# One stacked matmul for the gates' end tiles, transposes moved among the second halves, and a deeper lookahead

## The chip, the cores and the metric

The kernel runs on one core of a Trainium2 chip. The metric is the device time of one execution in microseconds. The kernel before took 1441.75 us (median of three runs, 1441.58 to 1443.41).

## The reference

The input is one sequence of 256 tokens of width 1024, in fp32. Two blocks follow one another, each two layers deep.

Each layer of the first block computes `proj = rmsnorm(x) @ w_in` and splits it for three branches: a gated spatial MLP (a), a latent attention (b) and a gated linear recurrence (c). Each branch's output is projected back to 1024 columns, multiplied by a sigmoid gate (`g_a`, `g_b`, `g_c`) and added up; the sum goes through `w_out` and a norm into the residual. The recurrence, which most of the change touches, is:

```python
r = sigmoid(blockdiag(xc, w_a) + b_a);  i = sigmoid(blockdiag(xc, w_x) + b_x)   # 16 blocks of 80 x 80
a = exp(-8 * r * softplus(-lam));       b = sqrt(1 - a*a) * (i * xc)
h[t] = a[t] * h[t-1] + b[t]             # along the 256 tokens;  y_c = h * silu(z_c)
```

The second block has a pooling mixer (first layer) or a sparse attention (second layer), then a convolutional feed-forward of inner width 2816, then a gate: `x = x + sigmoid(rmsnorm(x) @ ple_gate) * (p @ ple_proj)`. A last norm ends it.

## The kernel before, in words

**Arithmetic.** Every fp32 matrix product is made of three matmuls of rounded fp32 parts: `mm3` (L479 to L483) adds hi*hi, hi*lo and lo*hi. A product is either token-major (`tok_halves`, L569: the activations are stationary, 512 columns of weights stream; the 256 tokens are two halves of 128) or feature-major (`feat_tile`: the weights are stationary, 256 tokens stream).

**Weights.** All weights lie in one DRAM array in the order of use, in chunks of up to 512 KB. The class `Stream` loads them: `get` (L382) for chunk i first issues the loads up to chunk i + `raw_ahead` (3) and the splits up to i + `split_ahead` (2). A split (L364) is one ScalarE copy to `hi` (L376) and one VectorE subtraction per 512 columns to `lo` (L379). There are 4 raw buffers and 7 pairs of hi and lo; a raw buffer is free when VectorE has made its `lo`. All loads are issued by SyncE.

**Order.** The framework's scheduler takes the instructions of each engine mostly in the order in which the program gives them, lets a ready one pass one that waits (by its own model of time), and adds all semaphores. On the chip each engine then runs its list in order.

**Recurrence gates (`gates`, L944).** The 1280 channels are 10 tiles of 128, in two periods of 5 tiles, and the blocks of 80 straddle tiles. For each period, each of two gates and each of 5 tiles, there is one `mm3` on the tile itself and one on an `edge` operand with the neighbours' rows: 64 rows of the tile before and 64 of the one after, copied by GpSimd (L936) into `es` tiles. The two end tiles of a period (0 and 4) have one neighbour in the period, and take that neighbour's whole tile as `edge`. `MERGE_ORDER` runs branch a's gate and projection for one half of the columns (`ga`, `pa`), `gates(0)`, the other half, `gates(1)`.

**After the gates.** Both halves of the third gate's product (`gc`, on `hT`) come next; then VectorE squares `av` (L985), takes the minimum with 1 (L986), ScalarE the root (L987); VectorE multiplies (L989) and scans along the tokens (L992). Then `zc` (10 feature tiles, each pair with a silu at L617, L618, a product with the scan's result at L1001, and a split into `yc` at L491 and L492), then the projection `pc` on `yc` in two column halves of 5 chunks each.

**Feed-forward, gate, and their norms.** `ffn` ends with the last 7 inner tiles of the down product, half 0 of the tokens and then half 1. Then come, for each half, the residual (L1165), the next norm's product and sum of squares (L555, L512), eight transposes (L538, in the helper `transpose_split`) and the split into the next stage's `hT` (L488, L489). `tok_pair` (L579) computes the 1024-wide products with six chunks held, half 0 ahead of half 1; `ple` does its residual after it in the same manner.

Of the kernel before, what the change touches and what calls it, by code (L numbers as in the profile page):

```python
# [187 lines left out]
FFN_TAIL = 7  # L188
PAIR_HELD = 6
# [229 lines left out]
class Net:  # L419
# [59 lines left out]
    def mm3(self, ps, a, b, start, stop):  # L479
        mm = self.nc.tensor.matmul  # L480
        mm(ps, a[0], b[0], start=start, stop=False)  # L481
        mm(ps, a[0], b[1], start=False, stop=False)  # L482
        mm(ps, a[1], b[0], start=False, stop=stop)  # L483
# [59 lines left out]
    def norm(self, *key, dst=None, rs=None, fold=None):  # L543


        gain = self.row(*key)
        dst = dst or self.feat4("hT", KD)
        run_rs = rs or [None, None]

        def run(half):  # L550
            if fold:
                hs = self.u2s("h", 2)
                for n, h in enumerate(hs):
                    cs = slice(n * 512, (n + 1) * 512)
                    self.nc.vector.tensor_tensor(h, self.x[half][:, cs], gain[n], op=ALU.mult)  # L555
            if run_rs[half] is None:
                run_rs[half] = self.rs_x(half, fold or 1.0)
            if not fold:
                hs = self.scaled_x(half, run_rs[half], gain)
            for n, h in enumerate(hs):  # L560
                self.transpose_split(h, dst, half, 4 * n, 4)

        run.dst, self.rs = dst, run_rs
# [15 lines left out]
    def tok_pair(self, key, f):  # L579

        ps = [[self.psA(), self.psA()] for _ in range(2)]
        def part(half, i, w):
            n, c = divmod(i, 4)
            for k in range(2):
                kg = 2 * c + k
                self.mm3(ps[n][half], f.pair(kg, half), (w[0][:, k, :], w[1][:, k, :]), kg == 0, kg == KD - 1)

        def get(i):
            return self.w.get((*key, i // 4, i % 4), 512)

        ws = [get(i) for i in range(PAIR_HELD)]
        for i in range(PAIR_HELD):
            part(0, i, ws[i])
        for i in range(8 - PAIR_HELD):
            part(1, i, ws[i])
            ws.append(get(PAIR_HELD + i))
            part(0, PAIR_HELD + i, ws[-1])
        for i in range(8 - PAIR_HELD, 8):
            part(1, i, ws[i])
        return ps  # L600
# [132 lines left out]
    def first_layer(self, l):  # L733
# [119 lines left out]
        for n in range(2):  # L853
            ps = self.tok_group(("v", l, n), hT)
# [23 lines left out]
        for n in range(2):  # L878
            ps = self.tok_group(("u", l, n), hT)
            for half in range(2):  # L880
                nc.vector.tensor_tensor(sv[half][n], sv[half][n], ps[half], op=ALU.mult)
            heads(4 + 2 * n, 5 + 2 * n)
        ya = self.feat4("ya", 8)
        for n in range(2):
            ps = self.tok_group(("za", l, n), hT)
# [58 lines left out]
        def gates(p):  # L944
# [5 lines left out]
            for gi in range(2):  # L950
                pvs = []
                for mi in range(5):
# [6 lines left out]
                    self.mm3(pv, w[1], edge[mi], False, True)  # L959
# [14 lines left out]

        for kind, i in MERGE_ORDER:
# [4 lines left out]
        tg = [gate("gc", n) for n in range(2)]  # L980
# [135 lines left out]
    def ffn(self, l):  # L1116
# [26 lines left out]

        def down(*js):
            ws = [self.w.get(("down", l, j), 512) for j in js]
            for half in range(2):
                sl = slice(half * P, half * P + P)
                for j, (wh, wl) in zip(js, ws):
                    f = act[j]
                    for n in range(2):  # L1150
                        self.mm3(acc[half][n], (f[:, 0, sl], f[:, 1, sl]), (wh[:, n, :], wl[:, n, :]),
                                 j == 0, j == KF - 1)
# [8 lines left out]
        down(*range(KF - FFN_TAIL, KF))  # L1161
        for half in range(2):
# [3 lines left out]
            nxt(half)  # L1166
# [8 lines left out]
    def ple_in(self, l, n):  # L1175
        if n == 0:
            self.pp = [[], []]
        ps = self.tok_group(("pp", l, n), self.pf, kts=2)
# [5 lines left out]
    def ple(self, l):  # L1184
# [5 lines left out]
        pss = self.tok_pair(("pg", l), hT)  # L1190
        for half in range(2):
            for n in range(2):
                cs = slice(n * 512, n * 512 + 512)
                t = self.tmp()
                nc.scalar.activation(t, pss[n][half], AF.Tanh, scale=rs[half])
                nc.vector.scalar_tensor_tensor(t, t, 1.0, self.pp[half][n], op0=ALU.add, op1=ALU.mult)
                nc.vector.tensor_tensor(self.x[half][:, cs], self.x[half][:, cs], t, op=ALU.add)
            nxt(half)
# [15 lines left out]
    def nsa(self):  # L1214
# [15 lines left out]
        ps = self.tok_group(("kv", 0), h1)  # L1230
# [72 lines left out]
        def keys_values(s):  # L1303
            ps = self.tok_group(("kv", 1 + s), h1)
# [43 lines left out]
        def queries(n):  # L1348
            ps = self.tok_group(("qb", n), hT)
# [206 lines left out]
```

## Time and profile before

| | |
|---|---|
| median of 3 runs | 1441.75 us |
| profiled execution | 1441.76 us |
| its span, first to last instruction | 1440.0 us |
| TensorE / VectorE / ScalarE / GpSimd busy | 97% / 73% / 59% / 6% |
| granted TensorE clock, mean | 0.994 |
| DMA | 249.32 MB, mean 173 GB/s |
| chain that ended last | TensorE 81%, VectorE 9%, ScalarE 5%, DMA 3% |

The busy time of TensorE overstates its rate: a matmul's row gives its time from start to end, and the next one starts before that end. The pace is read from the starts in the timeline.

### The profile page before, as it was taken

To read this page: it belongs to the slowest core of one execution; us is meant where nothing else is said; L and a number is where in the kernel's file an instruction comes from. 1 tells how busy PE (TensorE), PEld (TensorE's weight loads), DVE (VectorE), ACT (ScalarE), POOL (GpSimd) and SP (SyncE) were. 2 spreads that over 40 slices of the span, in tenths; PEclk is the share of its full clock that TensorE was granted. 3 is DMA by queue.
4 is the path that set the end of the run, shared out by engine and by line. 5 is a ranking of instruction groups with operands and counts; after the bars stand their busy time and mean duration, and the time that the engine had idled before them with its cause. 6 is when DMAs were issued, how large, how long until landed. Compare 5 with 4: busy or idle time off the path is not lost.

```text
span 1440.0 us, 23026 instructions
## 1 busy us (share of the span) xinstructions
PE 1399.3 (97%) x8506; PEld 1236.1 (86%) x8506; DVE 1049.4 (73%) x2131; ACT 844.6 (59%) x1421; POOL 92.0 (6%) x155
## 2 busy tenths in 40 slices
PE   6999999999999999999999999999999999999997
PEld 6987889889789878898897899999888778999985
DVE  7856748659767676577687688777696788787765
ACT  6665545656455665456655466555565796665554
POOL 1000002100010000021000000000010440000000
PEclk9999999999999999999999999999999999999999
DMA  8553555564646634665656555555555115655652
GB/s 282 183 196 117 163 188 190 168 214 136 228 139 207 214 118 129 194 201 161 203 175 231 163 181 186 191 178 189 183 172 171 50 38 189 194 180 189 188 164 86
DMA packets 73408, 249.32 MB, mean 173 GB/s; under 512 B 8272, under 2 KB 8912, under 8 KB 73296
## 3 DMA queue, kind: packets, MB, share of 16 engines
q1 hardware_dynamic: 72576, 245.95, 52.1%
q10 hardware_dynamic: 720, 1.91, 0.5%
q8 instruction: 67, 1.10, 0.3%
q14 instruction: 45, 0.37, 0.1%
HBM read 246.77 MB, written 1.05 MB: 172 GB/s over the span
## 4 chain that ended last, share of the span: by engine, by line
PE 81%; DVE 9%; ACT 5%; DMA 3%; issue 2%; POOL 1%; POOLq 0%; ACTq 0%; DVEq 0%; SPq 0%
PE psA L481 22%; PE psA L483 22%; PE psA L482 22%; PE psB L481 3%; DVE lo L379 3%; PE psB L482 3%; DMA raw<-in_w_dram 3%; PE psB L483 3%; ACT hi L376 2%; PE psB L538 1%; ACT es L1415 1%; DVE av L992 1%; POOL rs L502 1%; PE psB L1054 1%; PE psB L1036 1%
## 5 line engine op out<-in xcount | busy, mean ns | idle before, releaser
L379 DVE TENSOR_TENSOR lo<-raw,hi 128x512 fp32r<-128x512 f32 (+2 forms) x897 | 585.0, 679 | 221.3 <-ACT hi L376 215.8
L376 ACT ACTIVATE hi<-raw 128x1024 fp32r<-128x1024 f32 (+3 forms) x449 | 467.6, 1045 | 309.8 <-PE psA L483 112.3
L482 PE MATMUL psA<-hT,hi 128*128 128x256 f32 x1160 | 328.6, 283 | 0.5 <-DVE hT L489 0.5
L483 PE MATMUL psA<-hT,lo 128*128 128x256 f32 x1160 | 328.2, 283 | 0.0
L481 PE MATMUL psA<-hT,hi 128*128 128x256 f32 x1160 | 328.1, 283 | 0.0
L481 PE MATMUL psA<-hi,hT 128*128 128x512 f32 (+2 forms) x592 | 230.6, 390 | 3.2 <-ACT hT L488 3.2
L482 PE MATMUL psA<-lo,hT 128*128 128x512 f32 (+2 forms) x592 | 228.5, 386 | 1.4 <-DVE lo L379 1.4
L483 PE MATMUL psA<-hi,hT 128*128 128x512 f32 (+2 forms) x592 | 229.1, 388 | 0.0
L482 PEld LDWEIGHTS psA<-hT,hi 128*128 128x128 f32 x1160 | 221.9, 191 | 2.0 <-DVE hT L489 0.7
L481 PEld LDWEIGHTS psA<-hT,hi 128*128 128x128 f32 x1160 | 221.8, 191 | 1.6 <-ACT hT L488 0.2
L483 PEld LDWEIGHTS psA<-hT,lo 128*128 128x128 f32 x1160 | 221.9, 191 | 0.0
L481 PEld LDWEIGHTS psA<-hi,hT 128*128 128x128 f32 x592 | 111.8, 189 | 22.6 <-ACT hT L488 4.1
L482 PEld LDWEIGHTS psA<-lo,hT 128*128 128x128 f32 x592 | 111.5, 188 | 21.4 <-DVE lo L379 2.1
L483 PEld LDWEIGHTS psA<-hi,hT 128*128 128x128 f32 x592 | 111.5, 188 | 20.4 <-DVE hT L489 0.5
L502 POOL TENSOR_TENSOR rs<-ms,mhalf 128x1 f32<-128x1 f32 x34 | 28.3, 832 | 977.1 <-DVE ms L501 788.1
L1135 DVE SCALAR_TENSOR_TENSOR tmp<-psA,colt,tmp 128x255 f32<-128x255 f32 (+1 forms) x176 | 84.2, 478 | 1.2
L481 PE MATMUL psB<-hi,fact 128*128 128x512 f32 x176 | 68.8, 391 | 0.0
L482 PE MATMUL psB<-lo,fact 128*128 128x512 f32 x176 | 68.8, 391 | 0.0
L483 PE MATMUL psB<-hi,fact 128*128 128x512 f32 x176 | 68.5, 389 | 0.0
L1132 ACT ACTIVATE tmp<-psA,colt 128x256 f32<-128x256 f32 x88 | 48.5, 551 | 1.9
L936 POOL CAST es<-xs 64x256 fp32r<-64x256 f32 x48 | 29.4, 640 | 270.1 <-ACT xs L488 269.3
L512 ACT ACTIVATE junk<-x 128x512 bf16<-128x512 f32 x36 | 22.6, 629 | 36.8 <-DVE x L1165 14.0
(342 smaller groups left out, 2238.1 us busy)
## 6 DMA issues: line engine op xcount, KB each, us to landing
raw<-in_w_dram SPq DMA_DIRECT2D x414, 512.0 KB, 3.6
raw<-in_w_dram SPq DMA_DIRECT2D x24, 384.0 KB, 3.8
row<-in_rows_dram SPq DMA_DIRECT2D x34, 256.0 KB, 5.4
raw<-in_w_dram SPq DMA_DIRECT2D x8, 448.0 KB, 3.2
raw<-in_w_dram SPq DMA_DIRECT2D x4, 480.0 KB, 3.3
x<-in_x_dram SPq DMA_DIRECT2D x4, 256.0 KB, 4.3
pm<-in_pm_dram ACTq DMA_DIRECT2D x2, 512.0 KB, 5.2
out_dram<-h SPq DMA_DIRECT2D x4, 256.0 KB, 2.1
```

The costliest lines, as they stand in the source:

```text
L376: self.nc.scalar.activation(hi[:, :n], t[:, :n], AF.Copy)
L379: self.nc.vector.tensor_tensor(lo[:, c], t[:, c], hi[:, c].bitcast(F32), op=ALU.subtract)
L481: mm(ps, a[0], b[0], start=start, stop=False)
L482: mm(ps, a[0], b[1], start=False, stop=False)
L483: mm(ps, a[1], b[0], start=False, stop=stop)
L502: nc.gpsimd.tensor_tensor(rs, ms, self.mhalf, op=ALU.pow)
L512: nc.scalar.activation(junk[:, :s.shape[1]], s, AF.Square, scale=float(n) ** -0.5 / mul, accum_out=ss[:, i:i + 1])
L538: nc.tensor.transpose(ps[:, i, :], src[:, (done + i) * P:(done + i + 1) * P], self.cf("ident"))
L936: nc.gpsimd.tensor_copy(edges[p][m][i][r], xs.pair(ct)[i][r].bitcast(F32))
L992: nc.vector.tensor_tensor_scan(ctile(av, ct), ctile(av, ct), ctile(xc, ct), 0.0, op0=ALU.mult, op1=ALU.add)
L1132: nc.scalar.activation(dst, src, AF.Identity, bias=self.col("fb", ct, l), scale=self.col("fw", 2 * 2 * KF + ct, l))
L1135: nc.vector.scalar_tensor_tensor(dst[:, s:], src[:, :S - s], self.col("fw", (2 - s) * 2 * KF + ct, l), dst[:, s:], op0=ALU.mult, op1=ALU.add)
```

## The change

The weights of an end tile's edge, of which 32 rows are not zero, are stacked three times into 96 rows; GpSimd replaces the third copy by the low part before use. The 32 rows of the neighbour are copied as hi, lo, hi into 96 rows of a new `es` tile. One matmul of 96 rows takes the place of the three. In the stretch from `MERGE_ORDER` to the second `gc`, the lookahead is 6 loads and 4 splits. `ga`, `pa` and `gc` go through a `tok_group` that takes both token halves chunk by chunk; the other callers of `tok_group` keep the old order under the name `tok_halves`. The squares move to ScalarE; squares, minima and roots come before the first half of `gc`, products and scans between its halves. The norms are split into `scale` and `turn` (the transposes); at the ends of `ffn` and of the first `ple`, half 0's `turn` is queued on TensorE behind a given matmul of half 1.

```diff
 def _band(wa, wx, period):
...
-            if m > 0:
-                out[64:, g, m, 1] = full[m * P - 64:m * P, m]
-            if m < 4:
-                out[:64, g, m, 1] = full[(m + 1) * P:(m + 1) * P + 64, m]
+            if m in (0, 4):
+                o = P if m == 0 else 4 * P - 32
+                for r in range(3):
+                    out[32 * r:32 * r + 32, g, m, 1] = full[o:o + 32, m]
+                continue
+            out[64:, g, m, 1] = full[m * P - 64:m * P, m]
+            out[:64, g, m, 1] = full[(m + 1) * P:(m + 1) * P + 64, m]
...
+FFN_LATE = 3
+PAIR_LATE = 4
...
     def tok_group(self, key, f, N=512, kts=KD, kper=2):
-        return list(self.tok_halves(key, f, N, kts, kper))
+        ps = [self.psA(), self.psA()]
+        for c in range(-(-kts // kper)):
+            wh, wl = self.w.get((*key, c), N)
+            for half in range(2):
+                for kg in range(c * kper, min(kts, (c + 1) * kper)):
+                    k = kg % kper
+                    self.mm3(ps[half][:, :N], f.pair(kg, half), (wh[:, k, :], wl[:, k, :]), kg == 0, kg == kts - 1)
+        return ps
...
+        if first:
+            first(0, [ps[0][0], ps[1][0]])
         for i in range(8 - PAIR_HELD, 8):
-            part(1, i, ws[i])
+            ins = part(1, i, ws[i])
+            if turn and i == 8 - PAIR_HELD + PAIR_LATE - 1:
+                with self.tc.issue_after(ins):
+                    turn(0)
+        if first:
+            first(1, [ps[0][1], ps[1][1]])
...
         def gate(gk, n):
             ts = []
-            for ps in self.tok_halves((gk, l, n), hT):
+            for ps in (self.tok_group if gk != "gb" else self.tok_halves)((gk, l, n), hT):
...
-            for half, ps in enumerate(self.tok_halves((pk, l, n), y, kts=kts)):
+            for half, ps in enumerate((self.tok_group if pk == "pa" else self.tok_halves)((pk, l, n), y, kts=kts)):
...
-            edges.append([xs.pair(5 * p + 1)] + [(e[:, :S], e[:, S:]) for e in es] + [xs.pair(5 * p + 3)])
+            ends = _k3(self.u2("es", F32R), S)
+            edges.append([ends[:96, 0]] + [(e[:, :S], e[:, S:]) for e in es] + [ends[:96, 1]])
...
+                if k in (1, 3):
+                    r = slice(0, 32) if k == 1 else slice(96, P)
+                    for i in range(3):
+                        nc.gpsimd.tensor_copy(edges[p][k // 3 * 4][32 * i:32 * i + 32],
+                                              xs.pair(ct)[i % 2][r].bitcast(F32))
...
                     self.mm3(pv, w[0], xs.pair(5 * p + mi), True, False)
-                    self.mm3(pv, w[1], edge[mi], False, True)
+                    if mi in (0, 4):
+                        wh, wl = w[1]
+                        nc.gpsimd.tensor_copy(wh[64:96], wl[64:96].bitcast(F32))
+                        nc.tensor.matmul(pv, wh[:96], edge[mi], start=False, stop=True)
+                    else:
+                        self.mm3(pv, w[1], edge[mi], False, True)
...
+        self.w.raw_ahead, self.w.split_ahead = 6, 4
         for kind, i in MERGE_ORDER:
...
-        tg = [gate("gc", n) for n in range(2)]
         tv = self.u2s("tv", 5)
...
         for j in range(5):
-            nc.vector.tensor_tensor(tv[j], av[j], av[j], op=ALU.mult)
+            nc.scalar.activation(tv[j], av[j], AF.Square)
             nc.vector.tensor_scalar(tv[j], tv[j], 1.0, None, op0=ALU.min)
+        for j in range(5):
             nc.scalar.activation(tv[j], tv[j], AF.Sqrt, bias=quarter, scale=-0.25)
+        tg = [gate("gc", 0)]
         for j in range(5):
             nc.vector.tensor_tensor(xc[j], xc[j], tv[j], op=ALU.mult)
...
+        tg.append(gate("gc", 1))
+        self.w.raw_ahead, self.w.split_ahead = 3, 2
...
     def ffn(self, l):
...
+        js = range(KF - FFN_TAIL, KF)
+        ws = [self.w.get(("down", l, j), 512) for j in js]
+        for half in range(2):
+            for j, w in zip(js, ws):
+                ins = down_one(j, half, w)
+                if half and j == KF - FFN_LATE:
+                    with self.tc.issue_after(ins):
+                        nxt.turn(0)
+            residual(half)
+        nxt.turn(1)
...
     def ple(self, l):
...
+        self.tok_pair(("pg", l), hT, residual, nxt.turn if l == 0 else None)
+        if l == 0:
+            nxt.turn(1)
```

`residual(half)` holds the same instructions as before, up to and with the norm's `scale`; in the second `ple` the last norm runs whole in it.

## Rows read from the trace of the kernel before

**Rows 1.** The page's busy time: engine, busy us, share, instructions.
```profile
PE   1399.3 (97%) x8506; PEld 1236.1 (86%) x8506; DVE 1049.4 (73%) x2131; ACT 844.6 (59%) x1421; POOL 92.0 (6%) x155
```

**Rows 2.** Stretches, layer 0: us, engines' busy (x), clock, DMA share, GB/s: gc, zc, pc.
```profile
306.60:328.40 21.80, 21.80 (x102) 18.22 (x101) 13.02 (x23) 12.43 (x16) 0.00 (x0) 1.00 0.57 188
328.40:356.20 27.80, 27.80 (x234) 27.80 (x234) 27.19 (x49) 16.46 (x22) 0.00 (x0) 1.00 0.41 135
365.50:368.90 3.40, 3.40 (x10) 2.66 (x9) 1.38 (x2) 0.04 (x1) 0.00 (x0) 0.51 0.92 253
```

**Rows 3.** Timeline (start us, us, engine, instruction): first gates matmul, first after.
```profile
269.43 0.28 PE L481 MATMUL psA<-xs,hi 128*128 128x256 f32 x1
...
276.62 0.40 PE L481 MATMUL psA<-hi,hT 128*128 128x512 f32 x1
```

**Rows 4.** Timeline of TensorE, layer 0's pc; idle before and its releaser in brackets.
```profile
360.74 0.39 PE L483 MATMUL psA<-hi,yc 128*128 128x512 f32 x1
...
361.42 0.39 PE L483 MATMUL psA<-hi,yc 128*128 128x512 f32 x1
363.69 0.50 PE L481 MATMUL psA<-hi,yc 128*128 128x512 f32 x1 [1.88 <-ACT yc L491]
...
369.22 0.40 PE L483 MATMUL psA<-hi,yc 128*128 128x512 f32 x1
```

**Rows 5.** Timeline of TensorE, layer 1's pc.
```profile
759.33 0.39 PE L483 MATMUL psA<-hi,yc 128*128 128x512 f32 x1
...
767.09 1.05 PE L481 MATMUL psA<-hi,yc 128*128 128x512 f32 x2
```

**Rows 6.** Timeline of ScalarE, layer 0's zc into pc.
```profile
353.94 1.06 ACT L376 ACTIVATE hi<-raw 128x1024 fp32r<-128x1024 f32 x1 [1.00 <-DMA raw<-in_w_dram]
...
360.40 0.58 ACT L617 ACTIVATE tmp<-psA 128x512 f32<-128x512 f32 x1
```

**Rows 7.** Groups by line, VectorE, zc of layer 0: xcount, busy us, mean ns, idle before.
```profile
L992 DVE TENSOR_TENSOR_SCAN av<-av,xc 128x256 f32<-128x256 f32 x10 | 6.1, 673 | 0.0
L985 DVE TENSOR_TENSOR tv<-av 128x512 f32<-128x512 f32 x5 | 3.3, 684 | 0.0
L989 DVE TENSOR_TENSOR xc<-xc,tv 128x512 f32<-128x512 f32 x5 | 3.2, 678 | 0.0
...
L986 DVE TENSOR_SCALAR tv<-tv 128x512 f32<-128x512 f32 x5 | 1.9, 419 | 0.0
```

**Rows 8.** Timeline of TensorE: ends of the first ffn, first ple, second ffn.
```profile
1025.79 1.04 PE L538 MATMUL psB<-cft,h 128*128 128x128 f32 x8
1027.23 0.50 PE L481 MATMUL psA<-hi,hT 128*128 128x512 f32 x1 [0.40 <-ACT hT L488]
...
1050.03 1.03 PE L538 MATMUL psB<-cft,h 128*128 128x128 f32 x8
1051.54 0.50 PE L481 MATMUL psA<-hi,hT 128*128 128x512 f32 x1 [0.47 <-ACT hT L488]
...
1406.14 1.03 PE L538 MATMUL psB<-cft,h 128*128 128x128 f32 x8
1408.43 0.50 PE L481 MATMUL psA<-hi,hT 128*128 128x512 f32 x1 [1.26 <-ACT hT L488]
```

**Rows 9.** The page's groups: GpSimd's edge copies.
```profile
L936 POOL CAST es<-xs 64x256 fp32r<-64x256 f32 x48 | 29.4, 640 | 270.1 <-ACT xs L488 269.3
```

**Rows 10.** Timeline of ScalarE, end of the first ffn: half 1's hT.
```profile
1029.73 0.59 ACT L488 ACTIVATE hT<-psB 128x512 fp32r<-128x512 f32 x1
```

**Rows 11.** Timeline of TensorE, sparse attention: a matmul of 80 rows and the next.
```profile
1187.10 0.40 PE L1445 MATMUL psB<-pcs,vc 80*128 80x512 f32 x1
1187.34 0.39 PE L481 MATMUL psA<-hi,yf 128*128 128x512 f32 x1
```

**Rows 12.** Timeline of VectorE: without and with GpSimd's copies beside it.
```profile
231.58 0.69 DVE L379 TENSOR_TENSOR lo<-raw,hi 128x512 fp32r<-128x512 f32 x1 [0.29 <-ACT hi L376]
...
232.79 0.89 DVE L379 TENSOR_TENSOR lo<-raw,hi 128x512 fp32r<-128x512 f32 x1
```

More of the change, by code (lines that the diff above doesn't have):

```diff
@@ L482, in mm3 @@
         mm(ps, a[0], b[1], start=False, stop=False)
-        mm(ps, a[1], b[0], start=False, stop=stop)
+        return mm(ps, a[1], b[0], start=False, stop=stop).ins
     def split(self, hi, lo, src, scale=None):
@@ L548, in norm, with scale @@
         run_rs = rs or [None, None]
-        def run(half):
+        hs = [None, None]
+        def scale(half):
             if fold:
-                hs = self.u2s("h", 2)
-                for n, h in enumerate(hs):
+                hs[half] = self.u2s("h", 2)
+                for n, h in enumerate(hs[half]):
                     cs = slice(n * 512, (n + 1) * 512)
@@ L558, in run, with turn @@
             if not fold:
-                hs = self.scaled_x(half, run_rs[half], gain)
-            for n, h in enumerate(hs):
+                hs[half] = self.scaled_x(half, run_rs[half], gain)
+        def turn(half):
+            for n, h in enumerate(hs[half]):
                 self.transpose_split(h, dst, half, 4 * n, 4)
+        def run(half):
+            scale(half)
+            turn(half)
+        run.scale, run.turn = scale, turn
         run.dst, self.rs = dst, run_rs
@@ L577, in tok_halves, with tok_pair @@
             yield ps[half]
-    def tok_pair(self, key, f):
+    def tok_pair(self, key, f, first=None, turn=None):
         ps = [[self.psA(), self.psA()] for _ in range(2)]
@@ L585, in part @@
                 kg = 2 * c + k
-                self.mm3(ps[n][half], f.pair(kg, half), (w[0][:, k, :], w[1][:, k, :]), kg == 0, kg == KD - 1)
+                ins = self.mm3(ps[n][half], f.pair(kg, half), (w[0][:, k, :], w[1][:, k, :]), kg == 0, kg == KD - 1)
+            return ins
         def get(i):
@@ L853, in first_layer @@
         for n in range(2):
-            ps = self.tok_group(("v", l, n), hT)
+            ps = list(self.tok_halves(("v", l, n), hT))
             for half in range(2):
@@ L878, in first_layer @@
         for n in range(2):
-            ps = self.tok_group(("u", l, n), hT)
+            ps = list(self.tok_halves(("u", l, n), hT))
             for half in range(2):
@@ L884, in first_layer @@
         for n in range(2):
-            ps = self.tok_group(("za", l, n), hT)
+            ps = list(self.tok_halves(("za", l, n), hT))
             for half in range(2):
@@ L1142, in up, with down_one @@
             act[j] = f
+        def down_one(j, half, w):
+            sl, f = slice(half * P, half * P + P), act[j]
+            for n in range(2):
+                ins = self.mm3(acc[half][n], (f[:, 0, sl], f[:, 1, sl]), (w[0][:, n, :], w[1][:, n, :]),
+                               j == 0, j == KF - 1)
+            return ins
         def down(*js):
@@ L1146, in down @@
             for half in range(2):
[L1147 to L1152, printed above, removed]
+                for j, w in zip(js, ws):
+                    down_one(j, half, w)
         for j in range(KF):
@@ L1160, in ffn, with residual @@
         nxt = self.norm("ple", l, fold=0.5)
-        down(*range(KF - FFN_TAIL, KF))
-        for half in range(2):
+        def residual(half):
             for n in range(2):
@@ L1165, in ffn @@
                 nc.vector.tensor_tensor(self.x[half][:, cs], self.x[half][:, cs], acc[half][n], op=ALU.add)
-            nxt(half)
+            nxt.scale(half)
+        js = range(KF - FFN_TAIL, KF)
+        ws = [self.w.get(("down", l, j), 512) for j in js]
+        for half in range(2):
+            for j, w in zip(js, ws):
+                ins = down_one(j, half, w)
[4 more added lines that the diff above has]
+        nxt.turn(1)
         self.hT = nxt.dst
@@ L1177, in ple_in @@
             self.pp = [[], []]
-        ps = self.tok_group(("pp", l, n), self.pf, kts=2)
+        ps = list(self.tok_halves(("pp", l, n), self.pf, kts=2))
         for half in range(2):
@@ L1189, in ple, with residual @@
         nxt = self.norm("nkv", fold=1.0) if l == 0 else self.final()
-        pss = self.tok_pair(("pg", l), hT)
-        for half in range(2):
+        def residual(half, pss):
             for n in range(2):
@@ L1194, in ple @@
                 t = self.tmp()
-                nc.scalar.activation(t, pss[n][half], AF.Tanh, scale=rs[half])
+                nc.scalar.activation(t, pss[n], AF.Tanh, scale=rs[half])
                 nc.vector.scalar_tensor_tensor(t, t, 1.0, self.pp[half][n], op0=ALU.add, op1=ALU.mult)
                 nc.vector.tensor_tensor(self.x[half][:, cs], self.x[half][:, cs], t, op=ALU.add)
-            nxt(half)
+            if l == 0:
+                nxt.scale(half)
+            else:
+                nxt(half)
+        self.tok_pair(("pg", l), hT, residual, nxt.turn if l == 0 else None)
+        if l == 0:
+            nxt.turn(1)
         self.hT = nxt.dst
@@ L1229, in nsa @@
             z.append(zt)
-        ps = self.tok_group(("kv", 0), h1)
+        ps = list(self.tok_halves(("kv", 0), h1))
         kv = []
@@ L1303, in keys_values @@
         def keys_values(s):
-            ps = self.tok_group(("kv", 1 + s), h1)
+            ps = list(self.tok_halves(("kv", 1 + s), h1))
             for half in range(2):
@@ L1348, in queries @@
         def queries(n):
-            ps = self.tok_group(("qb", n), hT)
+            ps = list(self.tok_halves(("qb", n), hT))
             for half in range(2):
```

## The prediction

> **What bounds the kernel now.** I read four views in this order. The page's busy shares come first: TensorE is busy 97% of the span and every other engine clearly less [rows 1], so a matmul taken out of a dense stretch is time gained, and beside that only places where TensorE waits can give anything. The table of stretches comes next: through `gc` and `zc` TensorE has no idle time at all, but in `zc` VectorE is busy 27.19 of 27.80 us and the DMA moves only 135 GB/s against 188 in `gc` [rows 2]. Then the timeline of TensorE, read by starts and not by durations: a 512-column matmul starts every (361.42 - 360.74) / 3 = 0.227 us though each lasts 0.39 [rows 4]. By that pace I looked for places where starts fall behind. In the parts that the change touches there are five: `pc` in both layers [rows 4, 5] and three stage ends [rows 8]. Last, the timeline of ScalarE ahead of the first of these, to see what came late [rows 6].
>
> **The stacked matmul.** A `gates` stage takes 276.62 - 269.43 = 7.19 us for 10 gate tiles of 6 matmuls, 0.120 us each [rows 3]. Two of three edge matmuls go, for 2 end tiles, 2 gates, 2 periods and 2 layers: 2 x 16 = 32 matmuls, 32 x 0.120 = 3.84 us, all in dense work. This is the sure term. It assumes that the 96-row matmul costs the same 0.120: a matmul of 80 rows is followed by the next after 0.24 us, where a full one takes 0.227 [rows 11]; over 16 of them that difference is 0.2 us, which I drop.
>
> The Trainium skill speaks against this: "TensorEngine Tiling (Array Packing)", Key Properties, says that changing the tiling mode drains the engine. Whether 96 rows is another mode no row here shows; if it were, what the pipelining hides would be lost at both borders of 16 matmuls, and the sum would be smaller by the amount under the rivals. The 0.24 us of [rows 11] speaks against a drain.
>
> The change adds GpSimd copies. Per layer there are 12 of 32x256 into the new edge tiles and 8 of 32x128 into the weights. The nearest row is 0.64 us for 64x256 [rows 9], so 20 x 0.64 = 12.8 us a layer on an engine that is busy 6% of the span. The edge copies are hidden by `ga` and `pa`, 96 matmuls x 0.227 = 21.8 us of TensorE work between the last `xc` and the first `gates`. The weight copies wait only for the chunk's split, which with four splits ahead is made before the stage begins; I cost them at nothing. If that cover is gone, each is a round trip before a matmul (a rival). Whether a copy into 32 rows of a weight tile must wait for matmuls that read other columns of the tile depends on how finely the waits are drawn. TensorE reads half 0 of `hT` from 1027.23 [rows 8], ahead of the write of half 1 into the same tile at 1029.73 [rows 10]: they are drawn by region, so it need not.
>
> **The stall at `pc`.** In layer 0, 15 starts from 361.42 to 369.22 take 7.80 us instead of 15 x 0.227 = 3.40: 4.40 us lost [rows 4]. Some 2.2 us are waits for `yc`; then the granted clock is 0.51 for the 3.40 us from 365.50 [rows 2], half of 2.4 GHz, which costs 3.40 / 2 = 1.7 us. In layer 1 16 starts from 759.33 to 767.09 take 7.76 us instead of 3.63: 4.13 us [rows 5]. Why is `yc` late? `pc` began 24 matmuls before the wait, at 361.65 - 24 x 0.227 = 356.2, so the last `zc` pair was ready for its silu then, but ScalarE starts it at 360.40 [rows 6], 4.2 us late, since splits ahead of it in the queue wait for DMA (1.00 us at 353.94). The DMA is late because raw buffers come free only when VectorE has made `lo`, and VectorE is full: the squares, minima, products and scans take 3.3 + 1.9 + 3.2 + 6.1 = 14.5 us in the `zc` stretch [rows 7].
>
> The change moves these 14.5 us into the `gc` stretch, and the squares (3.3 us) off VectorE. There VectorE would have 13.02 + 11.2 = 24.2 us of work in 21.8 [rows 2, 7]: 2.4 us spill into `zc`. In `zc` the load falls to 27.19 - 14.5 + 2.4 = 15.1 us; even with three more chunks split in it (6 x 0.68 = 4.1) it is 19.2 of 27.8. Then ScalarE does not wait for DMA; the last `yc` needs silu 0.58, two VectorE steps of 0.69, a copy of 0.6 and perhaps two subtractions in front, 4 us, against the 5.45 us that 24 matmuls cover. The wait goes, and the half clock with it: 4.40 + 4.13 = 8.5 us. What is late next is the first `zc` weights, which stand behind the scans on VectorE: from the end of `gates` these are 1.9 + 4 x 1.2 + 9.3 = 16 us of VectorE work, plus some 4 us of squares before, against 21.8 us of `gc`. It fits with about 2 us to spare, and that is the weak joint. On ScalarE squares, roots and two table loads are some 8 us; `gc`'s first four chunks are split before, which covers 4 x 6 x 2 x 0.227 = 10.9 us. The deeper lookahead itself I count at nothing: no row shows TensorE waiting for weights here. Its loads (6 ahead with 4 raw buffers) stand waiting in SyncE's queue, with only rows for later stages behind them.
>
> **The transposes among the second halves.** At three stage ends eight transposes start right after the last matmul, and the first product of the next stage follows 1.44, 1.51 and 2.29 us later [rows 8]. The transposes alone are 8 x (1.04 - 0.27) / 7 = 0.88 us at the mean single duration of 0.27; they stay. The remainder, waiting for the evictions, is 0.56 + 0.63 + 1.41 = 2.6 us, and is covered by the 12 matmuls (2.7 us) behind which half 0's eviction now runs. Half 1's own chain starts when it did, has fewer instructions in front of it on VectorE and ScalarE, and is covered by half 0's products, as now. If the transposes come before `h` is ready, TensorE waits there instead, so the value lies between -1 and 2.6; I take 2.6: at the feed-forward's end the transposes stand 30 of half 1's 42 matmuls, 6.8 us, behind half 0's last, and its two sums and two products need 4 x 0.69 = 2.8 us; in the gate it is 24 matmuls, 5.45 us, against that and two times two steps more, which is close.
>
> **Sum.** 3.84 + 8.5 + 2.6 = 14.9 us. The profiled execution took 1441.76 (span 1440.0 and 1.8 around it), the same as the median 1441.75. 1441.76 - 14.9 = 1426.9; I say 1427.
>
> **The rivals.**
> (1) `yc` stays late, or the lateness moves to the start of `zc`. For: VectorE is overbooked in `gc`, 24.2 in 21.8 us. Against: TensorE needs `zc`'s later chunks only 2.88 us apart. Without the 8.5 us: 1435.3.
> (2) The other side: the weight copy is in TensorE's path at each of 16 end tiles. A stop is the end of the matmul before, 0.28, the copy 0.64, the restart 0.10, less the 0.12 that it takes anyway: 0.90 us, 14.4 us in all, which gives 1441.3. The stops come four to a stage, 3.6 us of waiting; a wait of 2.2 us was followed by 1.7 us lost to the clock, so four stages add 6.8: 1448.1. It makes the kernel slower once a stop costs over 0.93 us. [Rows 8, 10] speak against it.
> (3) VectorE and GpSimd block each other. A subtraction beside the copies took 0.89 us instead of 0.69 [rows 12]. If each new edge copy held VectorE for its whole 0.64 us, 24 x 0.64 = 15.4 us of VectorE time are lost; where half of that comes out at TensorE: 1427 + 7.7 = 1434.7. By the row, 24 x 0.2 = 4.8 us, off the path. The Trainium skill, "SBUF — State Buffer", Who interferes with whom, has the strong form: an exclusive lock when VectorE has two SBUF inputs and GpSimd reads SBUF. The row shows a part of it.
> (4) The 96-row matmuls cost a fill of 0.283 - 0.120 = 0.16 us at both borders: 32 x 0.16 = 5.2, 1432.1.
> (5) The transposes gain nothing: 1429.5.
>
> **Chances.** Forecast 0.60, (1) 0.15, (2) 0.08, (3) 0.05, (4) 0.05, (5) 0.07. Its own range is 1424 to 1431; the upper end of the whole is drawn to 1437, over (1), (3) and (4), and the lower to 1423, if the transposes of half 1 come smoother too. A measurement here tells apart 0.2%, 2.9 us. All cases but (2) are faster by more; (2) is half no change, half slower. As two cases may meet, I give faster 0.87, same 0.06, slower 0.07.
>
> **What would show it.** Right: a `gates` stage of 52 x 0.120 = 6.2 us; no wait for `yc` at `pc` and a granted clock of 1.00 there; the first product on `hT` 0.23 us after the last matmul at the three stage ends; scans during `gc`. Wrong: TensorE released by GpSimd in `gates`, or waits for `lo` at the first `zc` tiles. A time over 1437 would mean that the order of work, not the count of matmuls, decided.

## The result and the profile after

The changed kernel took 1427.55 us, the median of four runs (1425.19 to 1429.14), against 1441.66 us for the kernel before: a ratio of 0.9899 [0.988, 0.9918]. Beside the experiments it ran twice more, at 0.9889 [0.9872, 0.9905] and 0.9898 [0.9885, 0.9912]. Over all twelve executions the mean is 1427.3 us, and over the 39 of the kernel before in the same comparisons 1442.3: 15.0 us are saved. The prediction said 1427, and 14.9. The profiled execution took 1429.07 us, with a span of 1427.3.

The busy times (engine, busy us, share, instructions) answer to [rows 1]:

```profile
PE 1393.6 (98%) x8474; PEld 1231.6 (86%) x8474; DVE 1046.5 (73%) x2121; ACT 848.8 (59%) x1431; POOL 114.1 (8%) x195
```

There are 32 matmuls fewer, and 40 GpSimd instructions more. The chain that ended last, by engine:

```profile
PE 86%; ACT 5%; DVE 4%; DMA 2%; issue 2%; POOL 1%; POOLq 0%; ACTq 0%; SPq 0%; DVEq 0%
```

VectorE has fallen from 9% to 4% in it, and TensorE risen from 81% to 86%.

The stretches of layer 0, in the columns of [rows 2] (busy us and count of TensorE, weight loads, VectorE, ScalarE, GpSimd; clock, DMA share, GB/s): `gc`, `zc`, the start of `pc`, and three stretches at half the clock:

```profile
304.12:326.40 22.28, 22.06 (x98) 17.94 (x97) 19.55 (x36) 18.45 (x26) 0.00 (x0) 1.00 0.30 99
326.40:355.20 28.80, 28.80 (x242) 28.79 (x240) 24.49 (x40) 17.90 (x23) 0.00 (x0) 1.00 0.82 269
355.20:369.00 13.80, 13.80 (x63) 11.44 (x62) 8.87 (x15) 6.42 (x7) 0.00 (x0) 1.00 0.57 198
410.40:413.80 3.40, 3.40 (x13) 3.40 (x12) 2.96 (x7) 1.20 (x5) 0.92 (x1) 0.50 0.43 133
813.10:816.50 3.40, 3.40 (x18) 3.40 (x18) 2.89 (x5) 1.55 (x2) 0.00 (x0) 0.50 0.90 242
1110.10:1113.50 3.40, 3.40 (x10) 1.83 (x10) 2.54 (x10) 3.37 (x18) 0.00 (x0) 0.50 0.00 0
```

In the kernel before `gc` starts at 305.60 and `zc` at 327.39, so the windows of [rows 2] begin 1.0 us late. Over the stages themselves, before:

```profile
305.60:327.39 21.79, 21.79 (x99) 18.03 (x97) 12.49 (x22) 12.62 (x16) 0.00 (x0) 1.00 0.53 175
327.39:356.18 28.79, 28.79 (x241) 28.79 (x240) 28.18 (x50) 17.27 (x22) 0.00 (x0) 1.00 0.43 142
```

`zc` is no longer VectorE's stage: 24.49 of 28.80 us where it was 28.18 of 28.79, and the DMA moves 269 GB/s instead of 142. `pc` starts at the full clock. The half clock now lies in two places where the profile of before did not have it, at 410.4 (the norm ahead of layer 1) and at 1110.1 (the sparse attention). The third, at 813.1 (the pooling stage), was there before as well.

The timeline of TensorE (start, length, instruction; in brackets the idle time before and what ended it): the second `gates` stage from its first matmul to the one behind it, the first matmul of `pc`, and the first on `ms` after it. It answers to [rows 3, 4]:

```profile
297.88 0.28 PE L487 MATMUL psA<-xs,hi 128*128 128x256 f32 x1
...
304.00 0.28 PE L998 MATMUL psA<-es,hi 96*128 96x256 f32 x1
304.12 0.40 PE L487 MATMUL psA<-hi,hT 128*128 128x512 f32 x1
...
355.20 0.40 PE L487 MATMUL psA<-hi,yc 128*128 128x512 f32 x1
...
384.71 0.50 PE L487 MATMUL psA<-hi,ms 128*128 128x512 f32 x1 [0.81 <-ACT ms L497]
```

A 96-row matmul is followed after 0.12 us, like any other of 256 columns. From the first matmul of `pc` to the first on `ms` it takes 384.71 - 355.20 = 29.51 us, with the same 132 matmuls and transposes that took 33.85 before. No wait for `yc` is left; at 355 the last silu of `zc` follows the start of `pc` by 356.29 - 355.20 = 1.1 us, where it was 4.2:

```profile
356.29 0.58 ACT L647 ACTIVATE tmp<-psA 128x512 f32<-128x512 f32 x1
```

One thing is new. The timeline of all engines in the middle of `gc`:

```profile
310.63 1.94 ACT L1029 ACTIVATE tv<-tv,quarter 128x512 f32<-128x512 f32 x3
...
311.36 2.43 DVE L1035 TENSOR_TENSOR_SCAN av<-av,xc 128x256 f32<-128x256 f32 x4
...
312.47 3.89 ACT L382 ACTIVATE hi<-raw 128x1024 fp32r<-128x1024 f32 x4
...
313.71 1.26 DVE L1032 TENSOR_TENSOR xc<-xc,tv 128x512 f32<-128x512 f32 x2
...
314.90 3.69 DVE L385 TENSOR_TENSOR lo<-raw,hi 128x512 fp32r<-128x512 f32 x6
...
315.63 0.50 PE L488 MATMUL psA<-lo,hT 128*128 128x512 f32 x1 [0.22 <-DVE lo L385]
```

ScalarE's roots hold the splits back until 312.47, VectorE then has scans and products ahead of the first `lo`, and the second column half of `gc` waits for it. By starts that costs 0.49 us in layer 0 and 0.50 in layer 1 (at 711.99).

At the ends of the first feed-forward, the first gate and the second feed-forward ([rows 8]) the transposes of half 0 now stand among half 1's matmuls. The lines show them at the first of the three, and at each the last matmul of the stage with the first product on `hT`:

```profile
1013.18 1.03 PE L544 MATMUL psB<-cft,h 128*128 128x128 f32 x8
1013.97 0.48 PE L487 MATMUL psB<-hi,fact 128*128 128x512 f32 x1
...
1016.56 0.39 PE L489 MATMUL psB<-hi,fact 128*128 128x512 f32 x1
1016.78 0.39 PE L487 MATMUL psA<-hi,hT 128*128 128x512 f32 x1
...
1040.25 0.39 PE L489 MATMUL psA<-hi,hT 128*128 128x512 f32 x1
1040.48 0.39 PE L487 MATMUL psA<-hi,hT 128*128 128x512 f32 x1
...
1395.71 0.39 PE L489 MATMUL psB<-hi,fact 128*128 128x512 f32 x1
1395.94 0.39 PE L487 MATMUL psA<-hi,hT 128*128 128x512 f32 x1
```

Eight transposes take 0.79 us from their start to the next matmul's. The first product on `hT` follows the stage's last matmul after 0.22 or 0.23 us, without a wait for an eviction.

### The profile page after: what moved, and what is told of

Its sections match the earlier page's. It is cut to its first block, busy times and chain, and to the rows that moved or that the text cites. A ratio compares the mean times of both kernels' runs of the same rounds, so it can differ in the third digit from the quotient of the medians.

```text
span 1427.3 us, 23014 instructions
## 1 busy us (share of the span) xinstructions
PE 1393.6 (98%) x8474; PEld 1231.6 (86%) x8474; DVE 1046.5 (73%) x2121; ACT 848.8 (59%) x1431; POOL 114.1 (8%) x195
## 4 chain that ended last, share of the span: by engine, by line
PE 86%; ACT 5%; DVE 4%; DMA 2%; issue 2%; POOL 1%; POOLq 0%; ACTq 0%; SPq 0%; DVEq 0%
PE psA L488 23%; PE psA L487 23%; PE psA L489 23%; PE psB L487 3%; PE psB L488 3%; PE psB L489 3%; DMA raw<-in_w_dram 2%; DVE lo L385 2%; ACT hi L382 1%; PE psB L544 1%; PE psB L1099 1%; PE psB L1081 1%; ACT es L1481 1%; POOL rs L508 1%; PE psA L1330 1%
```

## The experiments

My theory was the prediction's: three terms that add up, the stacked matmul, the stall at `pc`, and the transposes, with the lookahead of no account by itself. The rivals: GpSimd's copies take something back; the time comes from the lookahead or from the order of the token halves and not from the moved scans; the transposes gain nothing.

To judge single terms I read four stretches in each trace, by the starts of the same first and last matmul, so that all kernels have the same work between them but for the 16 matmuls a layer. S1 is from the first `gates` matmul to the first of `pc`, S2 from there to the first on `ms` (each for layers 0 / 1), S3 from the 60th down matmul before the end of the first feed-forward to the first scores of the sparse attention, S4 from the 60th before the end of the second to the last matmul. "Stages" is what the six stretches together save against the kernel before, in one profiled execution each; "saved" is the difference of the mean times in the same comparison, good to about 2 us by the intervals (the first row, with four runs on both sides, to 3): the same kernel gives 14.3, 16.1 and 14.5. Single terms are therefore judged by the stages.

| kernel | median us | ratio [95%] | saved | stages | S1 | S2 | S3 | S4 |
|---|---|---|---|---|---|---|---|---|
| before | 1441.66 | | | | 86.75 / 86.75 | 33.85 / 34.23 | 105.63 | 38.49 |
| changed | 1427.55 | 0.9899 [0.988, 0.9918] | 14.3 | 15.1 | 85.33 / 85.36 | 29.51 / 29.53 | 103.54 | 37.33 |
| c1_changed_again | 1426.34 | 0.9889 [0.9872, 0.9905] | 16.1 | 15.1 | 85.38 / 85.35 | 29.48 / 29.47 | 103.66 | 37.25 |
| c2_changed_third | 1428.04 | 0.9898 [0.9885, 0.9912] | 14.5 | 15.1 | 85.37 / 85.35 | 29.48 / 29.50 | 103.64 | 37.28 |
| e1_three_matmuls | 1430.11 | 0.992 [0.9908, 0.9932] | 11.6 | 12.0 | 86.75 / 86.75 | 29.65 / 29.51 | 103.65 | 37.38 |
| e2_scans_late | 1433.75 | 0.9943 [0.9929, 0.9956] | 8.4 | 6.9 | 84.83 / 84.83 | 34.35 / 33.84 | 103.68 | 37.31 |
| e3_turns_at_end | 1431.22 | 0.9925 [0.9912, 0.9937] | 10.9 | 12.5 | 85.35 / 85.40 | 29.55 / 29.50 | 105.11 | 38.25 |
| e4_lookahead_3_2 | 1429.57 | 0.9918 [0.9905, 0.9932] | 12.2 | 13.0 | 86.33 / 86.36 | 29.50 / 29.38 | 103.71 | 37.43 |
| e5_only_scans_early | 1440.76 | 0.9987 [0.9977, 0.9997] | 1.9 | 2.1 | 90.87 / 89.58 | 29.50 / 29.50 | 105.84 | 38.30 |
| e6_squares_on_vector | 1428.34 | 0.99 [0.9884, 0.9916] | 14.5 | 15.4 | 84.83 / 84.83 | 29.66 / 29.67 | 104.16 | 37.19 |
| e7_no_weight_copies | 1427.96 | 0.9899 [0.9883, 0.9916] | 14.5 | 14.8 | 85.35 / 85.38 | 29.57 / 29.58 | 103.70 | 37.31 |
| e8_merged_turns | 1425.56 | 0.9882 [0.9867, 0.9897] | 17.1 | 16.8 | 85.37 / 85.39 | 28.66 / 28.66 | 103.58 | 37.27 |
| e9_merged_turns_squares | 1425.79 | 0.988 [0.9866, 0.9893] | 17.2 | 17.2 | 84.83 / 84.83 | 28.65 / 28.65 | 104.03 | 37.51 |
| e10_halves_3_2 | 1432.24 | 0.9927 [0.9914, 0.9939] | 10.4 | 10.9 | 87.51 / 87.49 | 29.49 / 29.51 | 103.67 | 37.18 |

The two columns agree within 1.6 us in every row, so within that error the differences lie in these stretches. "Less saved" below is against the mean of the changed kernel's three comparisons, 15.0, unless the same comparison is named.

**The three matmuls back** (the layout of the weights goes back with them, and GpSimd's edge copies into the 96 rows go; the rest of the change stays):

```diff
-                    if mi in (0, 4):
-                        wh, wl = w[1]
-                        nc.gpsimd.tensor_copy(wh[64:96], wl[64:96].bitcast(F32))
-                        nc.tensor.matmul(pv, wh[:96], edge[mi], start=False, stop=True)
-                    else:
-                        self.mm3(pv, w[1], edge[mi], False, True)
+                    self.mm3(pv, w[1], edge[mi], False, True)
```

> The changed kernel with the end tiles' edges taken in three matmuls again (and without the GpSimd copies that belong to the stacking); all else as changed. Theory (the parts add up, each matmul costs its pace): 32 matmuls of 0.120 us come back, +3.84 us over the changed kernel, about 10.9 us less than before; a gates stage takes 7.2 us instead of 6.2. Rival (the stacking costs fills or GpSimd waits at its borders): less than +2 us, and gates stages of the changed kernel longer than 52 x 0.120. Either may be shifted by 1.7 us where a stretch of half clock comes or goes.

Measured 3.3 us less saved. The stage is back at 277.25 - 270.06 = 7.19 us:

```profile
270.06 0.28 PE L484 MATMUL psA<-xs,hi 128*128 128x256 f32 x1
...
277.25 0.40 PE L484 MATMUL psA<-hi,hT 128*128 128x512 f32 x1
```

S1 differs by 1.40 us a layer and not by 16 x 0.120 = 1.92: with the slower gates the wait in `gc` is gone, so 0.5 us of each layer's gain is given back there.

**Squares, minima, roots and scans after `gc` again**, with lookahead 3 and 2 from there on (the deep one ends ahead of the scans):

```diff
+        tg = [gate("gc", n) for n in range(2)]
+        self.w.raw_ahead, self.w.split_ahead = 3, 2
...
-        tg = [gate("gc", 0)]
...
-        tg.append(gate("gc", 1))
-        self.w.raw_ahead, self.w.split_ahead = 3, 2
```

(and one loop over j for square, minimum and root.)

> The changed kernel with both halves of gc ahead of squares, roots, products and scans again (the squares stay on ScalarE, the lookahead in the gates stretch stays deep). Theory (the place of VectorE's 11 to 14 us of work made yc late): the waits for yc at pc come back, with half clock behind them where they are 2 us long: +6 to +9 us over the changed kernel, less the 1.0 us of waits at the second half of gc. Rival (the deeper lookahead is what carries zc over): no wait at pc, within 2 us of the changed kernel.

Measured 6.6 us less saved. The waits for `yc` are back in both layers:

```profile
362.62 0.50 PE L487 MATMUL psA<-hi,yc 128*128 128x512 f32 x1 [1.88 <-ACT yc L497]
...
762.01 0.50 PE L487 MATMUL psA<-hi,yc 128*128 128x512 f32 x1 [1.27 <-ACT yc L497]
```

S2 is 4.9 and 4.3 us longer, S1 0.5 shorter in each layer, since nothing holds `gc` back. The stall at `pc` is the scans' place in VectorE's queue, and moving them costs `gc` 1.0 us in all.

**The transposes behind the last matmul again:**

```diff
-                if half and j == KF - FFN_LATE:
-                    with self.tc.issue_after(ins):
-                        nxt.turn(0)
+            if half:
+                with self.tc.issue_after(ins):
+                    nxt.turn(0)
```

(behind the loop over j; in `tok_pair` likewise.)

> The changed kernel with half 0's transposes behind the last matmul of half 1 again at the three stage ends. Theory: the first product on hT follows the first transpose by 1.4 to 2.3 us again, +2.6 to 3.5 us over the changed kernel, all at the two ends of ffn and that of the first ple. Rival (the wait is only moved to half 1's chain): no difference over 1 us.

Measured 4.0 us less saved; S3 and S4 are 1.6 and 0.9 longer than with the change, 2.5 in all. The waits for the eviction are those of [rows 8] again, two of them shorter:

```profile
1016.81 0.50 PE L487 MATMUL psA<-hi,hT 128*128 128x512 f32 x1 [0.25 <-ACT hT L494]
...
1041.14 0.50 PE L487 MATMUL psA<-hi,hT 128*128 128x512 f32 x1 [0.47 <-ACT hT L494]
...
1398.42 0.50 PE L487 MATMUL psA<-hi,hT 128*128 128x512 f32 x1 [1.02 <-ACT hT L494]
```

**The lookahead left at 3 and 2:**

```diff
-        self.w.raw_ahead, self.w.split_ahead = 6, 4
```

> The changed kernel with the lookahead of 3 loads and 2 splits throughout. Theory (predicted: the deeper lookahead is worth nothing where TensorE waited for no weights; it only covers ScalarE's squares and roots): ScalarE's 8 us of squares, roots and table loads now stand in front of the splits of gc's third chunk, 5.4 us after its start, so TensorE waits 2 to 4 us in each layer's gc, with half clock behind it in some: +4 to +11 us. Rival (free either way): within 1 us of the changed kernel. Rival (the lookahead removed the wait at pc): the waits for yc come back, +8 us, and none in gc.

Measured 2.7 us less saved, below the 4 to 11 expected. The stages show 2.0 of it, all in S1 (1.0 us a layer). `gc` now waits twice:

```profile
315.56 0.50 PE L488 MATMUL psA<-lo,hT 128*128 128x512 f32 x1 [0.22 <-DVE lo L385]
322.67 0.50 PE L488 MATMUL psA<-lo,hT 128*128 128x512 f32 x1 [0.70 <-DVE lo L385]
```

On ScalarE two splits stand ahead of the table load for the tanh, where the change has four (312.47 in the timeline above):

```profile
312.40 1.99 ACT L382 ACTIVATE hi<-raw 128x1024 fp32r<-128x1024 f32 x2
314.41 1.28 ACT L928 ACT_TABLE_LOAD   x1
```

So the deeper lookahead is worth 2 us by the stages, and my zero for it was wrong. No run took its loads and its splits apart.

**The kernel before with the move of the scans alone** (old lookahead, old order of the token halves, three matmuls, transposes at the end):

```diff
-        tg = [gate("gc", n) for n in range(2)]
...
-            nc.vector.tensor_tensor(tv[j], av[j], av[j], op=ALU.mult)
+            nc.scalar.activation(tv[j], av[j], AF.Square)
...
+        tg = [gate("gc", 0)]
...
+        tg.append(gate("gc", 1))
```

> The kernel before with one edit alone: squares (on ScalarE), minima and roots ahead of gc, products and scans between its halves; lookahead 3 and 2, halves one after the other, three matmuls, transposes at the end. Theory (the place of VectorE's work made yc late, and the lookahead covers ScalarE's squares and roots): no wait for yc at pc in either layer, some 5.5 us less waiting there; instead waits for lo of 1.5 to 4 us a layer in gc, so 1 to 4 us less than before. Rival (the deeper lookahead is needed for pc): the waits at pc stay.

Here the sum of separate terms falls: 1.9 us saved, 0.9987 [0.9977, 0.9997]. S2 is as short as with the whole change (9.1 us gained over both layers), but S1 grew by 4.1 and 2.8. The second column half of `gc` stops for its weights, and behind the stop the granted clock is 0.50 for the 3.40 us from 323.40 (in layer 0 alone):

```profile
318.21 2.95 ACT L376 ACTIVATE hi<-raw 128x1024 fp32r<-128x1024 f32 x3
318.52 2.43 DVE L993 TENSOR_TENSOR_SCAN av<-av,xc 128x256 f32<-128x256 f32 x4
319.94 0.39 PE L481 MATMUL psA<-hi,hT 128*128 128x512 f32 x1
320.87 0.67 DVE L990 TENSOR_TENSOR xc<-xc,tv 128x512 f32<-128x512 f32 x1
321.45 0.69 DVE L379 TENSOR_TENSOR lo<-raw,hi 128x512 fp32r<-128x512 f32 x1
322.19 0.50 PE L482 MATMUL psA<-lo,hT 128*128 128x512 f32 x1 [1.86 <-DVE lo L379]
323.96 0.79 PE L482 MATMUL psA<-lo,hT 128*128 128x512 f32 x1 [0.25 <-DVE lo L379]
```

In the old order the product of one token half runs through all four chunks in 24 matmuls, 5.4 us; chunk by chunk the same four last 48 matmuls, 10.9 us. ScalarE has some 6.5 us of work in those 5.4 (four splits of 1.0, a table load of 1.28, two tanh of 0.6), and still it is nearly in time: TensorE would have taken the third chunk's `lo` at 319.94 + 0.23 = 320.17, and the split of that chunk, the first of the three from 318.21, is made at some 319.3. Its subtraction needs 0.69 us, but starts at 321.45, behind four scans and a product. By the trace it is VectorE's queue that holds it.

**Halves in the old order with lookahead 3 and 2, the rest as changed:**

```diff
-            for ps in (self.tok_group if gk != "gb" else self.tok_halves)((gk, l, n), hT):
+            for ps in (self.tok_halves)((gk, l, n), hT):
...
-        self.w.raw_ahead, self.w.split_ahead = 6, 4
```

(`pa` likewise.)

> The changed kernel with ga, pa and gc taken one half after the other as before and the lookahead of 3 and 2 throughout. Theory (the move of the scans pays only if weights are split ahead of ScalarE's squares and roots; half 0 takes four chunks in 5.45 us, the chunk-by-chunk order in 10.9): waits for lo of 2 to 3 us a layer in gc, as in the scans' move alone, 4 to 7 us more than the changed kernel and 1 to 3 us more than with the lookahead alone taken back. Rival (the order of the halves does not matter): equal to the changed kernel with lookahead 3 and 2, 2 to 3 us more than the changed kernel.

Measured 4.1 us less saved than the changed kernel in the same comparison; the second wait of `gc` is twice as long as with the lookahead alone undone:

```profile
314.93 0.50 PE L488 MATMUL psA<-lo,hT 128*128 128x512 f32 x1 [0.23 <-DVE lo L385]
320.27 0.50 PE L488 MATMUL psA<-lo,hT 128*128 128x512 f32 x1 [1.38 <-DVE lo L385]
```

By S1 the lookahead carries 2.0 us of the whole, and the order by chunks another 2.3 (87.51 + 87.49 - 86.33 - 86.36). Against 84.83, a `gc` without waits, this kernel loses 5.3 us in S1; the scans' move alone lost 7.0, of which 1.7 is its half clock. The old order with the deep lookahead was not run.

**GpSimd's copies into the weights left out** (the third copy of the 32 weight rows stays the high part, so that product is another one):

```diff
-                        nc.gpsimd.tensor_copy(wh[64:96], wl[64:96].bitcast(F32))
```

> The changed kernel without GpSimd's copies into the stacked weights, so that the part of the sum with the weights' low part is left out. Theory (the copies are made ahead and cost nothing): within 0.7 us of the changed kernel once the clock is allowed for, gates stages equal within 0.1 us. Rival (a copy stands in TensorE's path): 0.9 us less at each of 16 end tiles.

Nothing moved in the stages: S1 is 85.35 / 85.38 against 85.33 / 85.36. The whole took 1.6 us more than the changed kernel in the same comparison, where its profile has one stretch of half clock more. The copies into the weights cost nothing that these stages show.

**The squares on VectorE as before:**

```diff
-            nc.scalar.activation(tv[j], av[j], AF.Square)
+            nc.vector.tensor_tensor(tv[j], av[j], av[j], op=ALU.mult)
```

> The changed kernel with the squares on VectorE again, in their new place. Theory (the new wait of 0.5 us a layer in the second half of gc is ScalarE's queue: squares, roots and a table load stand ahead of the split): ScalarE has 5 x 0.53 us less there, the wait goes, VectorE has 3.3 us more and carries it: 0 to 1 us less than the changed kernel. Rival (VectorE was the limit, so the squares had to leave it): waits for lo at gc or the first zc tiles, or for yc at pc, 2 us a layer and more.

The wait in `gc` goes (S1 84.83, which is 86.75 - 1.92), so the splits are in time: two of them stand where the squares stood, ahead of the roots' table load,

```profile
305.81 2.04 ACT L382 ACTIVATE hi<-raw 128x1024 fp32r<-128x1024 f32 x2
```

and their subtractions come ahead of the scans. The total does not follow: 14.5 us saved. 1.1 us are gained in S1; S2 loses 0.3 and S3 0.6, and the rest is within the error.

**The changed kernel again**, twice, as the measure for the others:

> The changed kernel itself, as a control beside the next three. Theory (stretches of half clock come after waits, but not after each wait and not in each execution): the same waits at the same places as in its first profile within 0.2 us, while the stretches of half clock may lie after others of them; median 1425 to 1429 us.

> The changed kernel once more, as a control beside the next three. Theory: the same waits within 0.2 us, and one to three stretches of half clock, each of which follows one of the waits that are left (the norm before layer 1, the pooling stage, the sparse attention); 1425 to 1429 us.

The six stretches repeat within 0.15 us. Not every wait does: the one ahead of layer 1 is 1.02, 0.74 and 1.13 us, where 0.2 was expected at most between them. What differs between executions is the half clock elsewhere: at 410 in the first profile, not in these two; in the pooling stage in the first two; in the sparse attention in the first and third.

**One step further: the transposes of the gated sum among `pc`'s second half.** After the change the first product on `ms` still waits for its eviction (0.81 us at 384.71 above). Twelve of the sixteen transposes go behind the matmuls of three inner tiles:

```diff
-        for n in range(2):
-            project("pc", n, yc, KL, tg[n])
-        for n in range(2):
-            for half in range(2):
-                self.transpose_split(merged[half][n], ms, half, 4 * n, 4, 0.5)
+        project("pc", 0, yc, KL, tg[0])
...
+                if half == 1 and kg in (1, 3, 6):
+                    th, tn = {1: (0, 0), 3: (1, 0), 6: (0, 1)}[kg]
+                    with self.tc.issue_after(ins):
+                        self.transpose_split(merged[th][tn], ms, th, 4 * tn, 4, 0.5)
...
+        self.transpose_split(merged[1][1], ms, 1, 4, 4, 0.5)
```

> The changed kernel with one more stage end done in the same way: of the merged columns' 16 transposes ahead of w_out, 12 run among the last half of pc, behind its second, fourth and seventh k tile, and the last 4 behind its end. Theory (as at the other stage ends, what goes is the wait for the eviction): the first matmul on ms comes 0.2 us after pc's last instead of 2.2 us (of which 1.3 are transposes that stay), 1.1 us less in each layer, 2.2 us in all. Rival (the last four transposes wait for VectorE's two steps on merged, in front of w_out): no gain, or up to 1 us lost a layer.

> The same, with the squares on VectorE as well. Theory (the wait of 0.5 us a layer in gc goes, as it did alone, and nothing takes its place): 0 to 1 us less than without it, 2.2 to 3.2 us less than the changed kernel. Rival (VectorE's further 3.3 us delay the merge at the end of pc): equal to it or slower.

```profile
378.47 0.60 PE L544 MATMUL psB<-cft,merged 128*128 128x128 f32 x4
...
383.28 0.39 PE L489 MATMUL psA<-hi,yc 128*128 128x512 f32 x1
383.51 0.40 PE L487 MATMUL psA<-hi,ms 128*128 128x512 f32 x1
```

The first product on `ms` starts 0.23 us after the last on `yc`, without a wait. The kernel took 1425.56 us, 0.9882 [0.9867, 0.9897], 2.6 us less than the changed kernel in the same comparison, of which S2 shows 0.83 a layer where 1.1 was expected. With the squares on VectorE as well it is the same within the error, 1425.79: `gc` gains its 1.1 us, S3 loses 0.4, much as with the squares alone. These two are the best versions run.

## Why the prediction was right, step by step

**The stacked matmul: right.** A `gates` stage takes 304.12 - 297.88 = 6.24 us, which is 52 x 0.120; S1 without a wait in `gc` is 86.75 - 84.83 = 1.92 us shorter, 3.84 over both layers. That the 96-row matmul costs no more than a full one is seen at 304.00. The Trainium skill's rule that a change of tiling mode drains the engine ("TensorEngine Tiling (Array Packing)", Key Properties) is not seen at work here: whatever 96 rows are to it, no drain is in these starts. In the sum the term is smaller, as `gc` takes 1.0 us of it back (below).

**The copies hidden: right.** By groups of lines (count, busy us, mean ns, idle before):

```profile
L967 POOL CAST es<-xs 32x256 fp32r<-32x256 f32 x24 | 15.4, 642 | 3.2 <-ACT xs L494 2.3
L997 POOL CAST hi<-lo 32x128 fp32r<-32x128 f32 x16 | 6.5, 427 | 46.4 <-DVE lo L385 46.1
```

I had taken 0.64 us for each; the copy of 32x256 took 0.642 and that of 32x128 0.427. In the run without the weight copies the stages are as long, so these cost nothing there. Rivals 2 and 4 fall by the unchanged pace. Rival 3 falls for the weight copies by that run, and for the edge copies by the run with three matmuls, which has none of them: from the 700th matmul ahead of the first `gates` to that stage it takes 129.09 us in both layers, against 129.13 and 129.15 with the copies. The effect behind it is there, but off the path: 28 subtractions that lay for over half their time beside one of GpSimd's casting copies took 0.78 us in the mean, the 828 beside none 0.69.

**The stall at `pc`: right in size, wrong in what it rests on.** 9.0 us came out of S2 where I had 8.5; rival 1 falls. The 0.5 is layer 1's: my count of starts ended at 767.09, while the half clock (0.50 from 764.90) lasts until 768.3. Yet the move of the scans pays only together with two edits that I priced at nothing, or not at all, the deeper lookahead and the order by chunks: "The deeper lookahead itself I count at nothing: no row shows TensorE waiting for weights here." No row did, because the scans were not there yet. Alone, the move gains 9.1 us in S2 and loses 7.0 in S1. I should have asked of `gc`, as I did of `zc`, how long four chunks last and what stands between two splits on ScalarE and VectorE.

**The weak joint: one stage too late.** I put it at the first `zc` weights, with 2 us to spare. `zc` has no idle TensorE time; the wait is in the second column half of `gc`, 1.0 us over both layers. ScalarE was busy with squares, table load and roots until 312.5, and VectorE took four scans and four products before the `lo` that TensorE wanted at 315.25. My cover of 10.9 us for ScalarE's 8 us was right for ScalarE alone and left out VectorE's queue behind it. VectorE's load in `zc` was 24.5 us, not 19.2, as fewer chunks were split during `gc`, where the DMA moved 99 GB/s: 28 subtractions stand in `zc` where before it had 15, and I had allowed for six more.

**The transposes: right.** 2.6 us predicted; undoing the edit alone costs 2.5 by S3 and S4, 4.0 by the times. The first product follows after 0.23 us, as said. Rival 5 (no gain) falls. S3 and S4 are 3.2 shorter than before, so some 0.8 us of that is not the place of the transposes: with them at the end again two of the waits for the eviction are still shorter, by 0.15 and 0.24 us, and the rest lies behind the first gate. What makes it no run shows.

**The clock: kept in part.** I had 3.4 us for two half-clock stretches at `pc`. Both are gone from `pc`. The two kernels that wait there, the one before and the one with the scans late, have three stretches of 3.4 us each in their profiles ahead of the end; the twelve profiles without that wait have 17, 1.4 on the average (3, 1 and 1 in the changed kernel's own). The 1.6 fewer are 2.7 us of the 3.4, at 1.7 us each. One profile of each kernel is little evidence, and the mean granted clock does not settle it, because 5 to 8 us at half the clock after the last matmul count in it and cost nothing.

**The sum.** By the stages 3.84 - 1.0 + 9.0 + 3.2 = 15.0, against 3.84 + 8.5 + 2.6 = 14.9: the wait that I missed, half a microsecond too little at `pc`, and the 0.8 us at the stage ends that I had not counted cancel. That the sum fits to 0.1 us is luck; that each term is near its own stretch is not.

## What to carry to other kernels

When work moves into a stage that shows no waits, check that stage's own supply: how long the weights in hand last in its order of work, and what is queued ahead of the next ones on each engine that prepares them. A change that only deepens a lookahead or reorders the use of chunks may gain nothing by itself and still be what another move stands on; price such edits together. Between same-looking kernels compare stretches from the same first to the same last instruction: they repeated within 0.15 us where whole executions spread by 4.

## What the runs showed of the hardware

The length of a wait did not tell whether the half clock followed. Ahead of layer 1 the first product waits for its `hT`; the first profile of the changed kernel (granted clock 0.50 from 410.40, above) shows

```profile
410.00 0.44 PE L487 MATMUL psA<-hi,hT 128*128 128x384 f32 x1 [1.02 <-ACT hT L494]
```

and the third one, which has a full clock there (1.00 over 410.70 to 414.10),

```profile
410.33 0.44 PE L487 MATMUL psA<-hi,hT 128*128 128x384 f32 x1 [1.13 <-ACT hT L494]
```

The longer wait had no half clock behind it. What decides it between two executions of one program stays open.

GpSimd's copies of 32x256 took 642 ns and those of 64x256 623 (640 in the kernel before): by these, half the rows save nothing, while half the columns do (32x128: 427).
